# Attention scores: the keys' remainder on all 128 rows, twice, and a second product that takes both parts of the query

## The chip, the core and the metric

The kernel runs on one core of one Trainium2 chip. The engines of the core run side by side, each through its own list of instructions in order: TensorE (PE, with its weight loads shown apart as PEld), VectorE (DVE), ScalarE (ACT), GpSimd (POOL) and SyncE (SP), which issues the transfers. The metric is the time of one execution on the device in microseconds (us); less is better.

## What is computed

Two layers of a backbone with 512 latent tokens and 256 context tokens, each 2048 wide. One projection feeds four groups of heads: a gating MLP, differential attention, a recurrence in two directions, and a short convolution. The change lies in the attention. Each of its four heads has two maps of 64 channels (m), and the two softmaxes are subtracted:

```python
def diff_attn_core(q, k, v, lam):
    s = _f32(jnp.einsum('bqhmd,bkhmd->bhmqk', q, k)) * (HD_QK ** -0.5)
    p = jax.nn.softmax(s, axis=-1)
    a = p[:, :, 0] - lam * p[:, :, 1]
    return jnp.einsum('bhqk,bkhd->bqhd', a.astype(v.dtype), v)
```

In layer 0 the context's queries attend to the 256 context keys and the latents' queries to all 768 keys. In layer 1 only the latents' queries are left.

## The kernel before

Large products are done in float32r, a type of matmul operand that holds a number less finely than float32. So an operand is split in two: a high part (the rounded copy) and a low part, the remainder (the number less its copy). A projection (`mtile`, `mstep`) multiplies three pairs of parts for each of 16 blocks of the contraction: high weights with the high part of h, high weights with the low part, low weights with the high part (line 306, tiles `wh`, `wl`, `h`, result `p`). The weights come by DMA as `wr`, ACT rounds them to `wh` (line 276), and POOL, or DVE for every fourth, subtracts to get `wl` (line 277). There are three buffers of `wh` and of `wl`.

The stages of a layer: the recurrence, then `groups_phase` (four heads of attention, four of the gating MLP, with two convolutions among them in layer 0), then the output projection. In `groups_phase` of layer 0, jobs of `gemv_dve` (line 222, DVE) are spread between the heads.

For one head, `attention` projects the queries and the keys, rotates them (`rot` on PE, line 959, and three elementwise operations, lines 961 to 963), and splits them by map. For map m the rounded channels go to 64 of the 128 rows of `q0` or `q1`, and the remainder of the query to the other 64 rows. Of the keys, `k0` and `k1` hold the rounded channels of their map twice, on both halves of the rows, and the one tile `klo` holds the remainders of both maps, map 0 on rows 0 to 63 and map 1 on rows 64 to 127. So the first product of a tile of scores (line 997) contracts over 128 rows and gives (high + low part of the query) times the high part of the key; the second (line 999) contracts over the 64 rows that `ms` picks, and adds high query times low key in the same PSUM tile `s`.

The loop over 128 queries (`qt`) has six steps in layer 0 (two for the context, with one part of 256 keys) and four in layer 1; a latent step has for each map two parts, 256 and 512 keys. There are 3 buffers of `s`. For each step DVE takes the maxima (lines 1001, 1004, 1005), ACT the exponentials (1008), DVE sums and reciprocals (1011, 1012, 1014), ACT scales the second map (1016), DVE combines both (1017); then PE transposes the result (1025), DVE and ACT copy it (1026), and PE multiplies it with the values (1029). The tile scheduler writes out the order of each engine when the program is built, and puts products of the next projections between the scores and the transposes.

Of the kernel before, what the change touches and what calls it, by code (L numbers as in the profile page):

```python
# [10 lines left out]
F32R = mybir.dt.float32r  # L11
# [92 lines left out]
class Kernel:  # L104
# [840 lines left out]
    def attention(self, l, h):  # L945
        nc, gp, der = self.nc, self.gp, self.der[l]
        V, G, A = nc.vector, nc.gpsimd, nc.scalar
        need_ctx = l < DEPTH - 1
        tT = lambda s, bufs=1, dt=F32: gp.tile([128, T], dt, tag=s, bufs=bufs, name=self.nm(s))

        qk = {}
        for s, c0 in (("q", 1536), ("k", 2048)):
            ctx = need_ctx or s == "k"
            p = self.proj(l, c0 + h * 128, ctx=ctx)
            x = tT("x")
            self.evac(x[:, 0:NCTX], x[:, NCTX:T], p)
            xl = x[:, NCTX:T]
            rp = self.pp.tile([128, 512], F32, tag="pp", name=self.nm("rot"))
            nc.tensor.matmul(out=rp, lhsT=self.rot, rhs=xl, start=True, stop=True)
            rs = gp.tile([128, NLAT], F32, tag="rs", name=self.nm("rs"))  # L960
            V.tensor_tensor(out=rs, in0=rp, in1=self.cs[:, 1, :], op=ALU.mult)
            G.tensor_tensor(out=xl, in0=xl, in1=self.cs[:, 0, :], op=ALU.mult)
            V.tensor_tensor(out=xl, in0=xl, in1=rs, op=ALU.add)
            cs = slice(0 if ctx else NCTX, T)
            t = qk[s] = [tT(f"{s}{m}", dt=F32R) for m in range(2)]
            if s == "k":
                klo = tT("klo", dt=F32R)
            for m, (a, b) in enumerate(((slice(0, 64), slice(64, 128)), (slice(64, 128), slice(0, 64)))):
                A.copy(out=t[m][a, cs], in_=x[a, cs])
                lo = t[m][b, cs] if s == "q" else klo[a, cs]  # L970
                V.tensor_tensor(out=lo, in0=x[a, cs], in1=t[m][a, cs], op=ALU.subtract)
                if s == "k":
                    A.copy(out=t[m][b, cs], in_=t[m][a, cs])
        p = self.proj(l, 2560 + h * 128)
        x = tT("x")
        self.evac(x[:, 0:NCTX], x[:, NCTX:T], p)
        vt = gp.tile([128, 6, 128], F32, tag="vt", name=self.nm("vt"))
        self.transpose6(x, vt, 0, lambda b0, b1, p: A.copy(out=vt[:, b0:b1, :], in_=p[:, 0:b1 - b0, :]))
        sg = self.gate2(gp, self.proj(l, 3072 + h * 128, ctx=need_ctx))

        o = tT("o")
        qt0 = 0 if need_ctx else 2
        for qt in range(qt0, 6):
            isctx = qt < 2
            nk = 2 if isctx else 6
            parts = ((0, NCTX),) if isctx else ((0, NCTX), (NCTX, NLAT))
            np_ = len(parts)
            e = []
            sm = gp.tile([128, 2, 6], F32, tag="sm", bufs=2, name=self.nm("sm"))
            for m in range(2):  # L990
                ms = slice(64 * m, 64 * m + 64)
                qs = slice(qt * 128, qt * 128 + 128)
                sps = []
                for i, (o0, n) in enumerate(parts):
                    s_ = self.sp.tile([128, 512], F32, tag="s", name=self.nm("s"))
                    ks = slice(o0, o0 + n)
                    nc.tensor.matmul(out=s_[:, 0:n], lhsT=qk["q"][m][:, qs], rhs=qk["k"][m][:, ks],
                                     start=True, stop=False)
                    nc.tensor.matmul(out=s_[:, 0:n], lhsT=qk["q"][m][ms, qs], rhs=klo[ms, ks],  # L999
                                     start=False, stop=True)  # L1000
                    V.tensor_reduce(out=sm[:, m, i:i + 1], in_=s_[:, 0:n], axis=AX.X, op=ALU.max)  # L1001
                    sps.append(s_)
                if np_ == 2:
                    V.tensor_tensor(out=sm[:, m, 0:1], in0=sm[:, m, 0:1], in1=sm[:, m, 1:2], op=ALU.max)
                V.tensor_scalar(out=sm[:, m, 2:3], in0=sm[:, m, 0:1], scalar1=-0.125, scalar2=None, op0=ALU.mult)  # L1005
                em = tT(f"e{m}")
                for i, (o0, n) in enumerate(parts):
                    A.activation(out=em[:, o0:o0 + n], in_=sps[i][:, 0:n], func=AF.Exp, scale=0.125,  # L1008
                                 bias=sm[:, m, 2:3], accum_out=sm[:, m, 3 + i:4 + i])
                if np_ == 2:  # L1010
                    V.tensor_tensor(out=sm[:, m, 3:4], in0=sm[:, m, 3:4], in1=sm[:, m, 4:5], op=ALU.add)
                V.reciprocal(out=sm[:, m, 5:6], in_=sm[:, m, 3:4])
                e.append(em)
            V.tensor_tensor(out=sm[:, 1, 5:6], in0=sm[:, 1, 5:6], in1=der["nlam"], op=ALU.mult)
            w = nk * 128
            A.activation(out=e[1][:, 0:w], in_=e[1][:, 0:w], func=AF.Copy, scale=sm[:, 1, 5:6])
            V.scalar_tensor_tensor(out=e[0][:, 0:w], in0=e[0][:, 0:w], scalar=sm[:, 0, 5:6], in1=e[1][:, 0:w],
                                   op0=ALU.mult, op1=ALU.add)
            aT = gp.tile([128, 6, 128], F32, tag="aT", bufs=1, name=self.nm("aT"))
            for b0, b1 in ((0, 2), (2, 6)):  # L1020
                if b0 >= nk:
                    continue
                p = self.pp.tile([128, 4, 128], F32, tag="pp", name=self.nm("atp"))
                for b in range(b0, b1):
                    nc.tensor.transpose(out=p[:, b - b0, :], in_=e[0][:, b * 128:(b + 1) * 128], identity=self.eye)
                (A.copy if b0 else V.tensor_copy)(out=aT[:, b0:b1, :], in_=p[:, 0:b1 - b0, :])
            op = self.pp.tile([128, 512], F32, tag="pp", name=self.nm("op"))
            for b in range(nk):
                nc.tensor.matmul(out=op[:, 0:128], lhsT=vt[:, b, :], rhs=aT[:, b, :], start=(b == 0),
                                 stop=(b == nk - 1))  # L1030
            A.copy(out=o[:, qt * 128:qt * 128 + 128], in_=op[:, 0:128])
        for o0, n in ((0, NCTX), (NCTX, NLAT)):
            if o0 < qt0 * 128:
                continue
            s = slice(o0, o0 + n)
            sq = gp.tile([128, NLAT], F32, tag="rs", name=self.nm("sq"))
            A.activation(out=sq[:, 0:n], in_=o[:, s], func=AF.Square)
            p = self.pp.tile([128, 512], F32, tag="pp", name=self.nm("ssq"))
            nc.tensor.matmul(out=p[:, 0:n], lhsT=self.ones, rhs=sq[:, 0:n], start=True, stop=True)
            A.activation(out=sq[:, 0:n], in_=p[:, 0:n], func=AF.Sqrt, scale=1.0 / 128, bias=self.eps[:, 0:1])  # L1040
            V.reciprocal(out=sq[:, 0:n], in_=sq[:, 0:n])
            V.tensor_tensor(out=o[:, s], in0=o[:, s], in1=sq[:, 0:n], op=ALU.mult)
            V.scalar_tensor_tensor(out=o[:, s], in0=o[:, s], scalar=der["sub"], in1=sg[:, s],
                                   op0=ALU.mult, op1=ALU.mult)
        nc.sync.dma_start(out=self.od[4 + h][:, qt0 * 128:T], in_=o[:, qt0 * 128:T])
# [247 lines left out]
```

## Time and profile before

| | us |
|---|---|
| median of 3 runs | 3791.88 |
| the runs | 3787.84 to 3800.24 |
| the profiled execution, its time on the device | 3795.03 |
| its span, first to last instruction | 3793.2 |
| PE busy in the span | 3508.6 |
| DVE / ACT / POOL busy | 2300.1 / 1866.6 / 1338.5 |

In the views a start is in us from the begin of the span. The duration of a matmul on PE reaches from its start to its modelled end, and matmuls overlap; what one costs in a stream is therefore read as the distance from its start to the start of the next. An x2 in a row of the timeline means two like instructions in a row.

### The profile page before, as it was taken

What the parts mean: (1) busy time and instruction counts of PE and PEld (TensorE: products, weight loads), DVE (VectorE), ACT (ScalarE), POOL (GpSimd) and SP (SyncE); (2) the same over time, 40 slices, a digit from 0 to 9 for tenths busy, and PEclk for the clock granted to TensorE, in tenths of its full rate; (3) what the DMA queues carried; (4) which work ended last, traced back from release to release, by engine and by line L of the source; (5) the groups of instructions that cost most, each with busy time, mean ns of one, the idle gap of its engine ahead of it and who ended that gap; (6) DMA issues with size and microseconds to landing.
All of it is one profiled execution on the core that took longest, in us unless ns stands there. A gap on an engine that the chain in (4) does not pass through costs nothing. (4 is left out here: it accounts for less than half of the span.)

```text
span 3793.2 us, 61920 instructions
## 1 busy us (share of the span) xinstructions
PE 3508.6 (92%) x22388; PEld 2829.0 (75%) x22388; DVE 2300.1 (61%) x4659; ACT 1866.6 (49%) x4131; POOL 1338.5 (35%) x1713
## 2 busy tenths in 40 slices
PE   6999999989999999999897899999778999999998
PEld 1477777767877877888776777777566787777797
DVE  5856777776376536463778734767667526643355
ACT  3466676765234344223324435767666524444454
POOL 2244444544222212222444433445334332222243
PEclk9999999989999999999999999999668999999999
DMA  8432222211343313343655433122011244422565
GB/s 299 181 114 66 58 65 67 62 44 44 104 120 95 98 57 95 109 139 119 201 158 184 124 110 93 55 66 63 27 29 45 64 148 129 123 62 81 158 194 180
DMA packets 239746, 400.89 MB, mean 106 GB/s; under 512 B 25936, under 2 KB 95568, under 8 KB 235344
## 3 DMA queue, kind: packets, MB, share of 16 engines
q1 hardware_dynamic: 232528, 386.45, 33.7%
q10 hardware_dynamic: 6912, 10.49, 0.8%
q8 instruction: 176, 2.88, 0.3%
q14 instruction: 130, 1.06, 0.1%
HBM read 363.28 MB, written 33.56 MB: 105 GB/s over the span
## 5 line engine op out<-in xcount | busy, mean ns | idle before, releaser
L306 PE MATMUL p<-h,wh 128*128 128x512 f32 (+3 forms) x8576 | 2175.9, 351 | 35.9 <-ACT y L1160 10.6
L306 PEld LDWEIGHTS p<-h,wh 128*128 128x128 f32 (+1 forms) x8576 | 1419.7, 191 | 250.6 <-issue 17.8
L306 PE MATMUL p<-h,wl 128*128 128x512 f32 (+2 forms) x4288 | 1350.8, 351 | 39.7 <-DVE wl L277 26.1
L277 POOL TENSOR_TENSOR wl<-wr,wh 128x512 fp32r<-128x512 f32 (+1 forms) x535 | 761.8, 1426 | 1606.5 <-ACT wh L276 1441.6
L276 ACT CAST wh<-wr 128x512 fp32r<-128x512 f32 (+1 forms) x756 | 466.5, 618 | 1001.0 <-PE p L306 792.3
L306 PEld LDWEIGHTS p<-h,wl 128*128 128x128 f32 (+1 forms) x4288 | 751.5, 191 | 143.2 <-DVE wl L277 32.8
L222 DVE SCALAR_TENSOR_TENSOR acc<-gw,sil,acc 128x512 f32<-128x512 f32 (+1 forms) x636 | 449.3, 763 | 33.4 <-DMA gw<-in_w_mod 31.2
L277 DVE TENSOR_TENSOR wl<-wr,wh 128x512 fp32r<-128x512 f32 (+1 forms) x221 | 160.6, 727 | 223.7 <-ACT wh L276 222.1
L804 PEld LDWEIGHTS <-ib 128*128 128x128 f16 x2304 | 133.7, 104 | 138.2 <-issue 70.9
L839 ACT CAST ib<-xa 64x256 f16<-64x256 f32 x480 | 176.4, 368 | 17.5 <-PE xa L809 11.7
L1001 DVE TENSOR_REDUCE sm<-s 128x1 f32<-128x256 f32 (+1 forms) x144 | 76.5, 542 | 102.0 <-PE s L999 99.5
L829 DVE TENSOR_TENSOR T<-inv,c 128x256 f16<-128x256 f32 x240 | 99.1, 413 | 37.0 <-PE inv L804 33.9
L741 POOL TENSOR_SCALAR sp<-SV,pcs 64x64 f32<-64x64 f32 x160 | 80.9, 510 | 108.1 <-DVE SV L762 83.4
L745 PE MATMUL ch<-SV,GM 128*128 128x128 f32 x384 | 90.0, 319 | 17.2 <-DVE SV L762 9.8
L652 POOL TENSOR_TENSOR bk<-t_tw,kr 64x256 f32<-64x256 f32 x96 | 92.7, 966 | 36.8 <-DVE kr L636 33.1
L1008 ACT ACTIVATE e<-s,sm 128x256 f32<-128x256 f32 (+1 forms) x144 | 80.9, 568 | 48.8 <-DVE sm L1005 39.4
L706 PE MATMUL g<-AR,BK 128*128 128x256 f32 (+1 forms) x384 | 96.0, 389 | 3.8 <-DVE BK L658 2.0
L748 PE MATMUL ch<-zs,xb 128*128 128x64 f32 x384 | 81.5, 297 | 15.2 <-ACT zs L747 13.8
L753 PE MATMUL ch<-UV,BKT 128*128 128x128 f32 x352 | 85.5, 328 | 10.2 <-ACT UV L750 9.2
L748 PEld LDWEIGHTS ch<-zs,xb 128*128 128x128 f32 x384 | 65.7, 204 | 38.8 <-ACT zs L747 32.7
L762 DVE SCALAR_TENSOR_TENSOR SV<-ch,pcs,sp 64x64 f32<-64x64 f32 x256 | 72.0, 281 | 36.7 <-PE ch L753 29.0
L835 ACT CAST X<-xa 128x256 f16<-128x256 f32 x192 | 71.4, 372 | 45.5 <-PE xa L809 43.0
(269 smaller groups left out, 5018.9 us busy)
## 6 DMA issues: line engine op xcount, KB each, us to landing
wr<-in_w_in SPq DMA_DIRECT2D x484, 256.0 KB, 2.7
wr<-in_w_out SPq DMA_DIRECT2D x256, 256.0 KB, 2.9
gw<-in_w_mod SPq DMA_DIRECT2D x192, 256.0 KB, 3.0
gw<-in_w_mod SPq DMA_DIRECT2D x32, 1024.0 KB, 6.7
gw<-in_w_mod SPq DMA_DIRECT2D x128, 128.0 KB, 3.1
raw<-rkvd SPq DMA_DIRECT2D x96, 128.5 KB, 2.1
lz<-lzd SPq DMA_DIRECT2D x48, 256.0 KB, 3.1
os<-od SPq DMA_DIRECT2D x32, 256.0 KB, 3.3
```

Of the source, the lines that this page charges most:

```text
L222: self.nc.vector.scalar_tensor_tensor(out=acc, in0=w, scalar=s, in1=acc, op0=ALU.mult, op1=ALU.add)
L276: self.nc.scalar.copy(out=hi, in_=raw)
L277: eng.tensor_tensor(out=lo, in0=raw, in1=hi, op=ALU.subtract)
L306: nc.tensor.matmul(out=p[0:w, 0:n], lhsT=a[:, kk, :], rhs=x[b][k], start=(first and kk == 0 and i == 0), stop=(last and kk == 3 and i == 2))
L652: G.tensor_tensor(out=bk[hs, :, h, :], in0=c4(an)[hs], in1=kn[hs], op=ALU.mult)
L706: nc.tensor.matmul(out=g[:, c], lhsT=bkc(c2 + c), rhs=AR[:, c2 + c, :, 0:nk, :], start=True, stop=True)
L745: nc.tensor.matmul(out=chp[:, 0:128], lhsT=two(GM[:, c, 0]), rhs=two(SV[:, c]), start=True, stop=True)
L748: nc.tensor.matmul(out=chp[:, 128:192], lhsT=XT32[:, c, :], rhs=zs, start=True, stop=True)
L753: nc.tensor.matmul(out=chp[:, 192:320], lhsT=BKT[:, c, :], rhs=two(UV[:, c]), start=True, stop=True)
L804: nc.tensor.matmul(out=out[:, c, :], lhsT=lhsT[:, c, :], rhs=rhs(c), **kw(c))
L829: V.tensor_tensor(out=T1, in0=p1, in1=bt(self.lm(d, j)), op=ALU.mult)
L839: A.copy(out=half(XT, h), in_=aXT[hs])
```

## The change

The keys' remainder gets two tiles, `klo0` and `klo1`, one for each map. DVE writes the 64 rows of the map as before, and a new GpSimd copy repeats them on the other 64 rows. The second product then takes the whole of `q0` or `q1` (128 rows) and the whole of `klo0` or `klo1`: it adds the low part of the query times the low part of the key, which was left out before.

```diff
             if s == "k":
-                klo = tT("klo", dt=F32R)
+                klo = [tT(f"klo{m}", dt=F32R) for m in range(2)]
             for m, (a, b) in enumerate(((slice(0, 64), slice(64, 128)), (slice(64, 128), slice(0, 64)))):
                 A.copy(out=t[m][a, cs], in_=x[a, cs])
-                lo = t[m][b, cs] if s == "q" else klo[a, cs]
+                lo = t[m][b, cs] if s == "q" else klo[m][a, cs]
                 V.tensor_tensor(out=lo, in0=x[a, cs], in1=t[m][a, cs], op=ALU.subtract)
                 if s == "k":
                     A.copy(out=t[m][b, cs], in_=t[m][a, cs])
+                    G.tensor_copy(out=klo[m][b, cs], in_=klo[m][a, cs])
...
-                ms = slice(64 * m, 64 * m + 64)
...
                     nc.tensor.matmul(out=s_[:, 0:n], lhsT=qk["q"][m][:, qs], rhs=qk["k"][m][:, ks],
                                      start=True, stop=False)
-                    nc.tensor.matmul(out=s_[:, 0:n], lhsT=qk["q"][m][ms, qs], rhs=klo[ms, ks],
+                    nc.tensor.matmul(out=s_[:, 0:n], lhsT=qk["q"][m][:, qs], rhs=klo[m][:, ks],
                                      start=False, stop=True)
```

On POOL two copies (line 974) come in for each head, 16 in all. This is POOL in the first head of layer 0, behind the rotation of the keys (line 962), before:

```order
L277 TENSOR_TENSOR wl_12646<-wr_12643,wh_12645 128x512
L277 TENSOR_TENSOR wl_12676<-wr_12673,wh_12675 128x512
L962 TENSOR_TENSOR x_12593<-x_12593,cs_12260 128x512
L277 TENSOR_TENSOR wl_12752<-wr_12749,wh_12751 128x512
L277 TENSOR_TENSOR wl_12782<-wr_12779,wh_12781 128x512
L277 TENSOR_TENSOR wl_12812<-wr_12809,wh_12811 128x512
```

And the same place of the changed kernel:

```order
L277 TENSOR_TENSOR wl_12649<-wr_12646,wh_12648 128x512
L277 TENSOR_TENSOR wl_12679<-wr_12676,wh_12678 128x512
L962 TENSOR_TENSOR x_12593<-x_12593,cs_12260 128x512
L974 COPY klo_2302_12604<-klo_2302_12604 64x768
L974 COPY klo_2303_12605<-klo_2303_12605 64x768
L277 TENSOR_TENSOR wl_12755<-wr_12752,wh_12754 128x512
L277 TENSOR_TENSOR wl_12785<-wr_12782,wh_12784 128x512
L277 TENSOR_TENSOR wl_12815<-wr_12812,wh_12814 128x512
```

The three splits of weights behind the rotation now stand behind the two copies, and the copies stand behind DVE's two subtractions (line 971), which they read.

On PE nothing moves. This is the begin of the scores in the last head of layer 1, before:

```order
L306 MATMUL p_36029<-h_21095,wl_36087 128x512
L997 MATMUL s_36107<-k_6660_35884,q_6641_35747 128x256
L999 MATMUL s_36107<-klo_35886,q_6641_35747 128x256
L997 MATMUL s_36111<-k_6660_35884,q_6641_35747 128x512
L999 MATMUL s_36111<-klo_35886,q_6641_35747 128x512
L997 MATMUL s_36122<-k_6661_35885,q_6642_35748 128x256
L999 MATMUL s_36122<-klo_35886,q_6642_35748 128x256
L306 MATMUL p_36334<-h_20990,wh_36337 128x512
```

And of the changed kernel:

```order
L306 MATMUL p_36053<-h_21107,wl_36111 128x512
L997 MATMUL s_36131<-k_6667_35905,q_6648_35768 128x256
L999 MATMUL s_36131<-klo_6669_35907,q_6648_35768 128x256
L997 MATMUL s_36135<-k_6667_35905,q_6648_35768 128x512
L999 MATMUL s_36135<-klo_6669_35907,q_6648_35768 128x512
L997 MATMUL s_36146<-k_6668_35906,q_6649_35769 128x256
L999 MATMUL s_36146<-klo_6670_35908,q_6649_35769 128x256
L306 MATMUL p_36358<-h_21002,wh_36361 128x512
```

The order is the same; the second product reads another tile, and its operands have 128 rows in place of 64. The orders of DVE, ACT and SP do not change either.

## Rows read from the trace of the kernel before

**Rows 1.** Busy time by stretch: us, PE, PEld, DVE, ACT, POOL, granted clock, DMA.

```profile
1030.00:1480.00 450.00, 437.31 (x2376) 356.95 (x2375) 273.93 (x514) 171.74 (x361) 104.40 (x69) 0.98 0.34 100
3140.00:3450.00 310.00, 304.92 (x1518) 235.18 (x1518) 161.79 (x340) 144.75 (x301) 73.95 (x54) 1.00 0.32 93
```

**Rows 2.** Chain of waits, 3140 to 3450 us: us in total, times, longest.

```profile
DVE sm L1001 <- PE s L999: 49.8, 36, 7.4
```

**Rows 3.** Groups by line and form, whole span: busy us, mean ns.

```profile
L999 PE MATMUL s<-klo,q 64*128 64x512 f32 x64 | 32.1, 502 | 0.0
L999 PE MATMUL s<-klo,q 64*128 64x256 f32 x80 | 30.9, 387 | 0.0
```

**Rows 4.** Timeline of PE: a stretch of products with 256 columns.

```profile
3387.69 0.28 PE L306 MATMUL p<-h,wl 128*128 128x256 f32 x1
3387.81 0.28 PE L306 MATMUL p<-h,wh 128*128 128x256 f32 x1
```

**Rows 5.** Timeline of PE at scores of the last head: start, us.

```profile
3406.51 0.39 PE L306 MATMUL p<-h,wl 128*128 128x512 f32 x1
3406.73 0.28 PE L997 MATMUL s<-k,q 128*128 128x256 f32 x1
3406.94 0.38 PE L999 MATMUL s<-klo,q 64*128 64x256 f32 x1
3407.25 0.49 PE L997 MATMUL s<-k,q 128*128 128x512 f32 x1
3407.68 0.50 PE L999 MATMUL s<-klo,q 64*128 64x512 f32 x1
3408.11 0.39 PE L997 MATMUL s<-k,q 128*128 128x256 f32 x1
3408.42 0.38 PE L999 MATMUL s<-klo,q 64*128 64x256 f32 x1
3408.73 0.74 PE L306 MATMUL p<-h,wh 128*128 128x512 f32 x2
3409.31 0.40 PE L306 MATMUL p<-h,wl 128*128 128x512 f32 x1
3409.55 0.63 PE L306 MATMUL p<-h,wh 128*128 128x512 f32 x2
3410.02 0.39 PE L306 MATMUL p<-h,wl 128*128 128x512 f32 x1
...
3410.93 0.40 PE L997 MATMUL s<-k,q 128*128 128x512 f32 x1
3411.26 0.50 PE L999 MATMUL s<-klo,q 64*128 64x512 f32 x1
```

**Rows 6.** Timeline of the weight loads there.

```profile
3406.51 0.19 PEld L997 LDWEIGHTS s<-k,q 128*128 128x128 f32 x1
3406.94 0.18 PEld L999 LDWEIGHTS s<-klo,q 64*128 64x128 f32 x1 [0.24 <-issue]
```

**Rows 7.** Timeline: the last scores before a transpose, and what it waits for.

```profile
3415.78 0.38 PE L999 MATMUL s<-klo,q 64*128 64x256 f32 x1
...
3418.05 1.02 DVE L1017 SCALAR_TENSOR_TENSOR e<-e,sm,e 128x768 f32<-128x768 f32 x1 [1.11 <-ACT e L1016]
...
3419.21 0.84 PE L1025 MATMUL atp<-cst,e 128*128 128x128 f32 x6
```

**Rows 8.** POOL's nearest operations, whole span, by form.

```profile
L652 POOL TENSOR_TENSOR bk<-t_tw,kr 64x256 f32<-64x256 f32 x96 | 92.7, 966 | 36.8 <-DVE kr L636 33.1
...
L861 POOL COPY GM<-AR 64x256 f32<-64x256 f32 x96 | 40.9, 426 | 130.9 <-PE inv L848 128.1 <-DVE lo L277 0.3
```

**Rows 9.** Timeline, first head of layer 0: DVE, POOL, PE.

```profile
1063.12 0.95 DVE L971 TENSOR_TENSOR klo<-x,k 64x768 fp32r<-64x768 f32 x1
...
1064.66 1.36 POOL L277 TENSOR_TENSOR wl<-wr,wh 128x512 fp32r<-128x512 f32 x1 [11.43 <-ACT wh L276]
...
1067.79 0.40 PE L306 MATMUL p<-h,wl 128*128 128x512 f32 x1
```

## The prediction

> **What bounds the kernel now.** I began with the busy time by stretch, around the two stages in which scores are made: the reader is to see PE at 437 of 450 us in layer 0 and at 305 of 310 us in layer 1, with DVE at 52 to 61%, ACT at 38 to 47% and POOL at 23 to 24%, and a granted clock of 0.98 to 1.00, which is the 2.4 GHz level [rows 1]. The waits agree: in layer 1 DVE's maxima waited 49.8 us in total for the second product of the scores (line 999) [rows 2]. So PE sets the time in these stages, and what a product costs in PE's stream is worth its full price until another chain takes over. The groups give the number of second products: 64 with 512 columns and 80 with 256, together 144 pairs, and their operands are 64 rows high, as nothing next to them is [rows 3].
>
> Then the timeline of PE, read as distances from start to start. In a stream of full-height float32r products one with 256 columns costs 0.12 us (3387.69 to 3387.81) [rows 4], one with 512 columns 0.22 to 0.23 us (3406.51 to 3406.73) [rows 5]. Around the 64-row products the same columns cost more [rows 5]:
>
> - The first product of a pair, behind full-height work: 256 columns 0.21 us (3406.73 to 3406.94), 512 columns 0.33 us (3410.93 to 3411.26). That is 0.09 to 0.10 over the stream.
> - The 64-row product: 256 columns 0.31 us (3406.94 to 3407.25, 3408.42 to 3408.73), 512 columns 0.43 us (3407.68 to 3408.11). That is 0.19 to 0.20 over.
> - The full-height product right behind it: as the first of the next pair it costs 0.43 us with 512 columns (3407.25 to 3407.68) and 0.31 us with 256 (3408.11 to 3408.42), that is 0.19 to 0.20 over, twice what a first product pays when no 64-row product precedes; and a projection's group of two costs 0.58 us (3408.73 to 3409.31) where the next such group costs 0.47 (3409.55 to 3410.02), 0.11 over. So 0.10 to 0.11 belongs to the way out of the 64-row product.
>
> The weight loads show why. The load for the first product starts at 3406.51, as the product before it starts and 0.22 us ahead of its own; the load for the 64-row product starts only at 3406.94, together with its own product, after 0.24 us in which the load side waited for nothing that the profile shows [rows 6]. The change of height stops the stream, twice a pair, and each time a load that is otherwise hidden is laid open.
>
> **The change part by part.** *The second product on 128 rows.* It becomes what line 306 issues in thousands: full height on full height, same type, same columns, into the same PSUM tile as the product before. I price it at the stream's 0.12 and 0.23 us. Then 0.09 + 0.19 + 0.11 = 0.39 us a pair goes. The run of three pairs at 3406.73 says the same: its seven products up to the group at 3408.73 are 0.09 + 0.19 + 0.20 + 0.20 + 0.19 + 0.19 + 0.11 = 1.17 us over the stream, 0.39 a pair [rows 5]. 144 pairs x 0.39 = 56 us. More rows for the same columns are priced at nothing: the first product has 128 rows and needs 0.21 us where the second with 64 rows needs 0.31.
>
> A rule speaks against this. A full-height weight load is seen to start with the product before it, of the same height [rows 5, 6]. The Trainium skill, "TensorE: Matmul & The Clock Gate", Part 3, The mechanism, says that a weight load overlaps products in flight only when its row group differs; two operands of 128 rows share every row group, so by that sentence alone the second load would stay open, and the saving would be near 0 in place of 56 us. The trace disagrees with that reading of it, in the load at 3406.51.
>
> *What is given back.* PE's order is fixed, and the transposes of a step (line 1025) wait for the softmax behind its scores. In the step shown the combination on DVE starts at 3418.05, lasts 1.02 and so ends at 3419.07, and the transposes start at 3419.21; the products put between keep PE occupied up to then, so there is no slack [rows 7]. The chain that ends there begins behind the pair whose second product starts at 3415.78. What PE saves up to that start moves the chain forward too; what it saves behind it (the way out, 0.19 + 0.11 = 0.30 us) does not, and PE will wait that long. There are 4 heads x (6 + 4) = 40 steps. Bounds: 0 if all have slack, and 40 x (0.30 + 0.39) = 28 us if none has and one whole pair more lies behind the start of the chain. I take 14 us, 0.35 a step: near the 0.30 of the row, with a little for the fourth tile of scores, which waits for one of three buffers.
>
> *The copies.* 16 copies of 64 x 768 on POOL, which is at a quarter of its time. The nearest row is POOL's copy of 64 x 256, 426 ns; three times the columns give about 1.3 us. The upper bound is its two-operand operation of that size, 966 ns, so 2.9 us [rows 8]. They cost POOL 20 to 46 us, and PE only if a split of weights behind them comes late. In the first head of layer 0 the second copy can start when DVE has the second remainder, at 1063.12 + 0.95 = 1064.07; at 1.3 us it ends at 1065.4, and the split that now starts at 1064.66 and lasts 1.36 ends at 1066.7. By program order it is first read by the product at 1067.79 [rows 9]. So the copies are hidden there with 1.1 us to spare. At 2.9 us each, and with both only behind 1064.07 (the first needs just the first remainder, so this is more than it can be), they would end at 1069.9 and the split at 1071.2, 3.4 us late; eight heads would give 27 us. I take 0, since a plain copy is what is issued. The scores start tens of us behind this place, so they do not wait for a copy.
>
> **Sum.** 56 - 14 - 0 = 42 us. The profiled execution took 3795.03 us (span 3793.2), which makes 3753. It lies 3.15 us above the median of the runs, 3791.88; against that the forecast is 3791.88 - 42 = **3750 us**, about 1.1% less.
>
> **The rivals.**
>
> - *The softmax chain takes over.* With PE faster, each step runs at the pace of maxima, exponentials and combination, and two or three of a latent step's four pairs are lost to waits. For it: the step of rows 7 has no slack. Against it: DVE and ACT are at about half in layer 1 [rows 1], and DVE's maxima wait for PE, not the other way [rows 2], so the chain itself starts earlier. It would gain 14 to 28 us: 3764 to 3778.
> - *Nothing is gained.* The load of the second product stays open at full height, as by the rule above; the distance from the second product stays at 0.31 and 0.43. Against it are the load at 3406.51 and every pair of products in rows 4 and 5. Time: 3792, within 0.3%.
> - *Slower, by POOL's queue.* The place is the pair of copies ahead of the splits, in every head. To eat 42 us and make the kernel 11 us slower (0.3%, about what a measurement of this kernel can tell from no change), PE would have to stand 53 / 8 = 6.6 us in each head. From 1064.07 to the product at 1067.79 there are 3.7 us, of which the split needs 1.4 [rows 9]; with both copies behind 1064.07 they would have to last 2.3 + 6.6 = 8.9 us, 4.5 each. That is over three times what the nearest copy gives, and above the bound of 2.9. It decides from there on; at 2.5 us each, by the same working, PE stands 2.7 us a head and half of the forecast is gone. Time at 4.5 us: 3803.
>
> **How the numbers follow.** The forecast with its bounds, 28 to 57 us gained (3735 to 3764), gets 0.81; the softmax chain 0.11; nothing gained 0.04; slower 0.02; more than 57 us, if the stream also tightens elsewhere, 0.02. Faster by over 0.3% then holds the first, the second and the last: 0.94; same 0.04; slower 0.02. The range is 3735 to 3768: the bounds of the forecast, with a few us of the chain's case or of late splits at the upper end.
>
> **What would show it.** In the profile after, the distance from a second product to the next start is 0.12 us at 256 columns and 0.23 at 512, and that from a first product too; the weight load of line 999 starts before its product, with no 0.24 us of idle ahead of it. Line 974 has 16 copies on POOL at 1.2 to 1.4 us. The waits show more in front of line 1025, some 0.3 us a step, behind line 1017. The stages named in rows 1 are shorter, with some 56% of the gain in layer 0, which has 80 of the 144 pairs; all others are as they were. What would make it wrong: second products at 0.31 and 0.43 still; a wait for `wl` behind the copies of a microsecond or more in each head; or waits in front of line 1025 or for buffers of `s` that add up to over 28 us.

## The result and the profile after

The changed kernel takes 3745.28 us (median of 4 runs, 3740.13 to 3750.04) against 3791.22 us for the kernel before beside it: a ratio of 0.9875, 95% interval 0.9853 to 0.9896, so 45.9 us or 1.25% less. The forecast was 3750 us.

First the place that was priced, the scores in the last head of layer 1, in the timeline of PE after the change (start, duration in us); it answers to [rows 5]:

```profile
3356.11 0.39 PE L306 MATMUL p<-h,wl 128*128 128x512 f32 x1
3356.33 0.28 PE L997 MATMUL s<-k,q 128*128 128x256 f32 x1
3356.45 0.28 PE L999 MATMUL s<-klo,q 128*128 128x256 f32 x1
3356.57 0.40 PE L997 MATMUL s<-k,q 128*128 128x512 f32 x1
3356.80 0.40 PE L999 MATMUL s<-klo,q 128*128 128x512 f32 x1
3357.03 0.28 PE L997 MATMUL s<-k,q 128*128 128x256 f32 x1
3357.15 0.27 PE L999 MATMUL s<-klo,q 128*128 128x256 f32 x1
3357.26 0.63 PE L306 MATMUL p<-h,wh 128*128 128x512 f32 x2
3357.73 0.39 PE L306 MATMUL p<-h,wl 128*128 128x512 f32 x1
```

Six products take 0.93 us (3356.33 to 3357.26) where they took 2.00 (3406.73 to 3408.73). Every product with 256 columns costs 0.11 to 0.12 us to the next start, every one with 512 costs 0.23, and the projection's group of two costs 0.47 again.

The weight loads of such a pair a little later, which answer to [rows 6] (after the arrow, who ended the idle time of the load side):

```profile
3359.34 0.19 PEld L997 LDWEIGHTS s<-k,q 128*128 128x128 f32 x1 [0.29 <-ACT e L1008]
3359.45 0.19 PEld L999 LDWEIGHTS s<-klo,q 128*128 128x128 f32 x1
```

The second load starts 0.11 us behind the first, while the product that it feeds starts only at 3359.68. It is hidden. The first one shows what was rare before: it waits for an exponential (line 1008), that is for one of the three buffers of `s`, and starts together with its product. In the timeline of PE:

```profile
3359.34 0.50 PE L997 MATMUL s<-k,q 128*128 128x512 f32 x1
3359.68 0.39 PE L999 MATMUL s<-klo,q 128*128 128x512 f32 x1
```

That product costs 0.34 us to the next start, where the one at 3356.57, of the same 512 columns, costs 0.23: a load laid open costs 0.11 us here, with no change of height near it.

By lines 997 and 1029, from the source view by layer (count, min/median/max ns, first and last start), the two score stages can be measured in both kernels. Before:

```profile
L997 PE MATMUL s<-k,q x80: 274/386/628, 1086.2 to 1510.0; 128*128 128x256 f32 x48, 128*128 128x512 f32 x32
L1029 PE MATMUL op<-aT,vt x224: 270/275/377, 1099.6 to 1518.7; 128*128 128x128 f32 x112
L997 PE MATMUL s<-k,q x64: 276/388/495, 3159.3 to 3444.4; 128*128 128x256 f32 x32, 128*128 128x512 f32 x32
L1029 PE MATMUL op<-aT,vt x192: 270/275/377, 3173.7 to 3453.0; 128*128 128x128 f32 x192
```

After:

```profile
L997 PE MATMUL s<-k,q x80: 278/371/498, 1079.9 to 1477.1; 128*128 128x256 f32 x48, 128*128 128x512 f32 x32
L1029 PE MATMUL op<-aT,vt x224: 270/275/377, 1088.1 to 1485.6; 128*128 128x128 f32 x112
L997 PE MATMUL s<-k,q x64: 277/340/505, 3123.5 to 3389.3; 128*128 128x256 f32 x32, 128*128 128x512 f32 x32
L1029 PE MATMUL op<-aT,vt x192: 270/275/377, 3136.4 to 3397.7; 128*128 128x128 f32 x192
```

From the first score to the last product with the values, layer 0 goes from 1518.7 - 1086.2 = 432.5 to 405.7 us and layer 1 from 293.7 to 274.2: together 726.2 to 679.9, 46.3 us less. That is about the whole of the change in the medians (45.9 us). The two profiled executions (3795.03 and 3740.13 us) differ by 54.9; the 8.6 us outside the score stages lie in stages that the change does not touch, and this rest moves about as much between the seven profiles of this study that share PE's order (3058 to 3068 us).

### The profile page after: what moved, and what is told of

Read it like the earlier page. It is cut to its first block, busy times and chain, and to the rows that moved or that the text cites. A ratio compares the mean times of both kernels' runs of the same rounds, so it can differ in the third digit from the quotient of the medians.

```text
span 3738.3 us, 61946 instructions
## 1 busy us (share of the span) xinstructions
PE 3448.6 (92%) x22388; PEld 2811.2 (75%) x22388; DVE 2303.8 (62%) x4659; ACT 1863.0 (50%) x4131; POOL 1364.5 (36%) x1729
## 5 line engine op out<-in xcount | busy, mean ns | idle before, releaser
L222 DVE SCALAR_TENSOR_TENSOR acc<-gw,sil,acc 128x512 f32<-128x512 f32 (+1 forms) x636 | 458.5, 778 | 27.4 <-DMA gw<-in_w_mod 25.1
L745 PEld LDWEIGHTS ch<-SV,GM 128*128 128x128 f32 x384 | 64.4, 204 | 37.6 <-issue 9.3
```

The costliest lines, as they stand in the source:

```text
L222: self.nc.vector.scalar_tensor_tensor(out=acc, in0=w, scalar=s, in1=acc, op0=ALU.mult, op1=ALU.add)
L745: nc.tensor.matmul(out=chp[:, 0:128], lhsT=two(GM[:, c, 0]), rhs=two(SV[:, c]), start=True, stop=True)
```

## The experiments

All ratios are to the kernel before. Beside the times, the table gives the two score stages of each profile, measured as above. Layer 1 is a steadier measure than the whole time; layer 0 is less so, for the clock moves it. `copies_only` has PE's order and products of the kernel before and is 4.5 us shorter there; its granted clock averages 0.996 over that stage, against 0.984 before and 0.992 in the changed kernel, the rest of the time being at the 1.2 GHz level. In the trace before, each of the three stretches at that level begins in a wait of PE of 1.9 to 2.9 us at the begin of a head, or within 1.5 us behind one. By an estimate (the length of the stage times the share that the clock lacks) that is at the most 1.7, 6.8 and 3.4 us, so some 3 of the 46.3 us may be clock and not change; against `copies_only` the two stages are 42.4 us shorter.

| kernel | median us | ratio (95% interval) | layer 0 | layer 1 | both |
|---|---|---|---|---|---|
| before | 3786 to 3791 | 1 | 432.5 | 293.7 | 726.2 |
| changed | 3745.28 | 0.9875 (0.9853 to 0.9896) | 405.7 | 274.2 | 679.9 |
| copies_only | 3785.95 | 0.9997 (0.9982 to 1.0012) | 428.0 | 294.3 | 722.3 |
| zero_half | 3749.53 | 0.9899 (0.9882 to 0.9917) | 406.1 | 275.2 | 681.3 |
| second_twice | 3810.30 | 1.0070 (1.0053 to 1.0087) | 446.1 | 299.3 | 745.4 |
| rows96 | 3741.18 (one run) | | 404.3 | 275.4 | 679.7 |
| no_second | 3736.07 | 0.9861 (0.9824 to 0.9898) | 406.8 | 273.7 | 680.5 |
| copies_twice | 3748.84 | 0.9897 (0.9867 to 0.9926) | 410.2 | 274.7 | 684.9 |
| inverse_rows128 | 3743.82 | 0.9882 (0.9856 to 0.9908) | 408.1 | 274.5 | 682.6 |

Theory 1 is that of the prediction: PE's stream stops when the height of the operands changes between 64 and 128 rows. The rivals say that the gain is from something else in the change, or that a 64-row product is slow by itself.

**One half of the change at a time.** `copies_only` has the tiles and the copies, with the product on 64 rows:

```diff
-                    nc.tensor.matmul(out=s_[:, 0:n], lhsT=qk["q"][m][:, qs], rhs=klo[m][:, ks],
+                    nc.tensor.matmul(out=s_[:, 0:n], lhsT=qk["q"][m][64 * m:64 * m + 64, qs], rhs=klo[m][64 * m:64 * m + 64, ks],
```

> Only half of the change: two tiles of the keys' remainder and the 16 GpSimd copies, but the second product still takes 64 rows. Theory 1 (the change of height stops PE's stream): all 144 pairs keep their 0.39 us, so 3791 us within 5, and the second product still costs 0.31 and 0.43 us to the next start. Rival (the gain comes from something else that the change brings, such as where tiles lie): about 3745. If the copies cost PE time, this run is later than 3791, by up to 27.

It is the kernel before in time (3785.95 us, where the kernel before beside it took 3788.27), and in its last head the second products cost 0.31 to 0.32 us (256 columns) and 0.43 us (512 columns), in the timeline of PE:

```profile
3395.77 0.28 PE L997 MATMUL s<-k,q 128*128 128x256 f32 x1
3395.97 0.38 PE L999 MATMUL s<-klo,q 64*128 64x256 f32 x1
3396.29 0.49 PE L997 MATMUL s<-k,q 128*128 128x512 f32 x1
3396.71 0.50 PE L999 MATMUL s<-klo,q 64*128 64x512 f32 x1
3397.14 0.39 PE L997 MATMUL s<-k,q 128*128 128x256 f32 x1
```

`zero_half` has the product on 128 rows without the copies (the tiles are made once a layer):

```diff
+            for m in range(2):
+                nc.gpsimd.memset(self.klo[m][64 * (1 - m):64 * (1 - m) + 64, :].bitcast(F32), 0.0)
...
-                klo = [tT(f"klo{m}", dt=F32R) for m in range(2)]
+                klo = self.klo
...
-                    G.tensor_copy(out=klo[m][b, cs], in_=klo[m][a, cs])
```

> The other half: second product on 128 rows, but no copies; each tile of the remainder is kept for the layer and its other half is set to zero once, so the low part of the query adds nothing there. Theory 1: 3745 us within 4, with the second product at 0.12 and 0.23 us. If the 16 copies cost the changed kernel time, this run is under 3745, by up to 10 us.

At 3749.53 us it lies just above the forecast of 3745 within 4; its ratio overlaps with that of the changed kernel, and its score stages are within 1.4 us of it. So the taller product alone makes the gain, the copies alone make none, and it does not matter what the other 64 rows hold.

**The copies, doubled.** `copies_twice` repeats the line with `G.tensor_copy`.

```diff
+                    G.tensor_copy(out=klo[m][b, cs], in_=klo[m][a, cs])
```

> The changed kernel with each GpSimd copy made twice (32 in place of 16, some 1.2 us each). If the copies are hidden, 3745 us within 4. If they already hold PE up, 16 x 1.2 = 19 us more, about 3764.

Of 19 us of further work on POOL, 3.6 us appear in the median and 5.0 in the score stages (4.5 of them in layer 0, 0.5 in layer 1), both no more than the runs scatter. The interval of its ratio alone reaches just far enough to hold the 19 us (0.9926); the half of a microsecond in layer 1 leaves no room for it, nor do the waits: PE stands 2.2 us (layer 0) and 1.0 us (layer 1) for `wl` from POOL, each time in the first head of the layer and ahead of its first scores, and in no other head. The copies are nearly hidden.

**What stops the stream.** `second_twice` is the kernel before with the 64-row product issued a second time (line 1001 of that file), which adds the low part of the key twice:

```diff
                     nc.tensor.matmul(out=s_[:, 0:n], lhsT=qk["q"][m][ms, qs], rhs=klo[ms, ks],
+                                     start=False, stop=False)
+                    nc.tensor.matmul(out=s_[:, 0:n], lhsT=qk["q"][m][ms, qs], rhs=klo[ms, ks],
                                      start=False, stop=True)
```

> The kernel before with the 64-row product issued twice in a row (the keys' remainder is added twice). Theory 1: the first of the two follows one of the same height and streams at 0.12 and 0.23 us; 80 x 0.12 + 64 x 0.23 = 24 us of work come in, so 3805 to 3815. Rival (a 64-row product costs 0.31 and 0.43 us wherever it stands): 80 x 0.31 + 64 x 0.43 = 52 us, so 3830 to 3843.

The time is as theory 1 said, but the distances are not. The timeline of PE:

```profile
3415.18 0.28 PE L997 MATMUL s<-k,q 128*128 128x256 f32 x1
3415.38 0.38 PE L999 MATMUL s<-klo,q 64*128 64x256 f32 x1
3415.61 0.28 PE L1001 MATMUL s<-klo,q 64*128 64x256 f32 x1
3415.81 0.50 PE L997 MATMUL s<-k,q 128*128 128x512 f32 x1
3416.24 0.49 PE L999 MATMUL s<-klo,q 64*128 64x512 f32 x1
3416.58 0.39 PE L1001 MATMUL s<-klo,q 64*128 64x512 f32 x1
3416.91 0.38 PE L997 MATMUL s<-k,q 128*128 128x256 f32 x1
```

With 256 columns the first 64-row product costs 0.23 us (3415.38 to 3415.61) and the second 0.20; with 512 columns 0.34 and 0.33. Neither streams at 0.12 and 0.23, and neither costs the 0.31 and 0.43 of the kernel before. Both fit one rule: a change of height, in either direction, costs about 0.09 us at the change, and the product behind the change costs 0.11 us more whatever comes next. The 0.11 is what a load laid open costs in the changed kernel too (3359.34). Here it is the load of the first 64-row product, which starts with its product, in the timeline of the weight loads; the next load starts 0.11 us behind it:

```profile
3415.38 0.18 PEld L999 LDWEIGHTS s<-klo,q 64*128 64x128 f32 x1 [0.24 <-issue]
3415.49 0.19 PEld L1001 LDWEIGHTS s<-klo,q 64*128 64x128 f32 x1
```

What the engine does in the 0.09 us no run shows. In the kernel before a 64-row product is both behind a change and ahead of one, so it bears 0.09 + 0.11 = 0.20 us; here the two halves fall on two products. Each tile of scores has two changes, 0.40 us, with one 64-row product or with two: summed over all of them and the products right behind, the distances lie 62 us over the stream in both traces. (The scheduler orders PE's work a little differently in this kernel, with 18 products of line 306 fewer in the stages, so its stages are no clean measure of the time that came in.)

The Trainium skill, "TensorEngine Tiling (Array Packing)", Key Properties, has this as a drain of the engine at a change of the tiling mode. The runs agree and give its price here.

`rows96` asks whether any other number of rows does it; for map 1 it leaves out half of the rounded query rows:

```diff
-                    nc.tensor.matmul(out=s_[:, 0:n], lhsT=qk["q"][m][:, qs], rhs=klo[m][:, ks],
+                    nc.tensor.matmul(out=s_[:, 0:n], lhsT=qk["q"][m][0:96, qs], rhs=klo[m][0:96, ks],
```

> The changed kernel with the second product on rows 0 to 95 (for map 1 half of the rounded query rows are left out). If any other number of rows stops the stream: 0.31 and 0.43 us for the second product, and 3790 us. If only half the height does, and 96 rows count as full height: 0.12 and 0.23 us, and 3745.

In its one run it is the changed kernel in time, and its timeline of PE has full speed between 128 and 96 rows:

```profile
3358.16 0.28 PE L997 MATMUL s<-k,q 128*128 128x256 f32 x1
3358.28 0.29 PE L999 MATMUL s<-klo,q 96*128 96x256 f32 x1
3358.40 0.40 PE L997 MATMUL s<-k,q 128*128 128x512 f32 x1
3358.64 0.40 PE L999 MATMUL s<-klo,q 96*128 96x512 f32 x1
3358.87 0.28 PE L997 MATMUL s<-k,q 128*128 128x256 f32 x1
```

So theory 1 holds in its narrow form: it is the half height that stops the stream, not just any number of rows that differs: 96, the only other one tried, does not.

**The same cure elsewhere.** `inverse_rows128` tries it on the 64 x 64 products of the recurrence (line 809), on top of the changed kernel:

```diff
-        xs = lambda h, hs, c: XT[hs, c, 64 * h:64 * h + 64]
+        xs = lambda h, hs, c: XT[:, c, 64 * h:64 * h + 64]
...
-        mm1(aXT, lambda h, hs, c: self.eyeh[hs], xs, part(no, no))
+        mm1(aXT, lambda h, hs, c: self.eyeh, xs, part(no, no))
...
-            mm1(aXT, lambda h, hs, c: T1[hs, c, :], xs, part(no, lambda c: j == 5 and c == 3))
+            mm1(aXT, lambda h, hs, c: T1[:, c, :], xs, part(no, lambda c: j == 5 and c == 3))
```

> The changed kernel, and in the inverse of the recurrence the 64 x 64 float16 products (line 809) take all 128 rows, where the other operand is zero on the other half: the same result, 64 columns of weights as before. If the half height alone stops the stream, some 240 groups lose two stops of 0.1 to 0.2 us each, 48 to 96 us of PE's time, of which a stage that often waits for other engines passes on less than half: 3700 to 3730. If the half width of the output stops it too, no change: 3745 within 4.

The time did not move. The groups by form of the changed kernel and, in the second fence, of this one:

```profile
L809 PE MATMUL xa<-ib,T 64*64 64x64 f16 x1920 | 79.5, 205 | 1.4 <-DVE T L829 1.4
```

```profile
L809 PE MATMUL xa<-ib,T 128*64 128x64 f16 x1920 | 80.3, 209 | 1.4 <-DVE T L829 1.4
```

The products are 128 rows high now but still fill 64 columns of the array, and the stop stays: the median distance from the last 128 x 128 product (line 804) to the first of line 809 is 0.123 us in both traces (242 places), where line 804 to itself takes 0.029. It is not the change of line, tile or type: from line 804 with 64 columns to line 306, full height and full width, the median is 0.029 us as well (159 places). The half width stops the stream as the half height does.

**How far PE still sets the pace.** `no_second` leaves out the low part of the key altogether:

```diff
                     nc.tensor.matmul(out=s_[:, 0:n], lhsT=qk["q"][m][:, qs], rhs=qk["k"][m][:, ks],
-                                     start=True, stop=False)
-                    nc.tensor.matmul(out=s_[:, 0:n], lhsT=qk["q"][m][ms, qs], rhs=klo[ms, ks],
-                                     start=False, stop=True)
+                                     start=True, stop=True)
```

> The kernel before without the second product at all: the low part of the key is left out of the scores. Against the changed kernel another 80 x 0.12 + 64 x 0.23 = 24 us of PE's work go. If PE still sets the pace in the score stages of the changed kernel, four fifths or more of that come through: 3722 to 3727. If the softmax chain has taken over there, little does: 3738 to 3745.

It comes out at 3736 us, between the two forecasts. That is 9 us under the changed kernel by the medians and 5 us by the ratios, with intervals that overlap; the score stages are 680.5 us long, no shorter than 679.9. So a gain from a further 24 us of PE's work is not shown. What took its place is only partly known. The scheduler arranges PE's order anew when the products go: other rows move too, and 29 more products of line 306 fall inside the stages, an estimated 5.5 us at the stream's distances. The granted clock over the stage in layer 0 averages 0.975, against 0.992 in the changed kernel, by the same estimate as above up to 7 us more. And the longest wait of PE in layer 0 is then for ACT's copies out of PSUM at the heads' begin:

```profile
PE p L306 <- ACT x L331: 12.1, 2, 6.1
```

In the changed kernel the same wait is 4.8 us. So the run brings in losses of its own and does not tell what PE's pace is still worth; that the softmax holds PE up in most steps is read from the changed kernel itself, in the next section.

## Why the prediction was right

**The saving per pair was right.** 0.39 us x 144 = 56 us was forecast. Summed over all 144 pairs and the products right behind them, the distances from start to start lie 62.2 us over a stream of 0.117 and 0.227 us in the trace before and 7.3 us over it in the trace after: 54.9 us less. (That the two profiled executions differ by the same 54.9 us is chance.) Of the 7.3 us that are left, 4.8 lie at first products with 512 columns, as the one at 3359.34. 80 of the 144 pairs are in layer 0, and 26.8 of the 46.3 us were gained there (58%, forecast 56%; against `copies_only` 22.3 of 42.4, 53%).

**Its division was not.** The prediction read 0.09 us for the way in, 0.19 to 0.20 for the way out, and 0.11 for the product behind it. `second_twice` shows two equal stops of 0.09 + 0.11; the way out seemed dear because the 64-row product pays the second part of its own entry. The sum of a pair is the same, so the forecast did not suffer, but for two 64-row products in a row the prediction's reading gives wrong distances.

**What is given back was priced too high, at the right place.** This is the term of the sum that was mis-sized. 54.9 us of distances became 46.3 us of stage: 8.6 us lost, where 14 were taken (bounds 0 and 28). Over the 40 steps the product ahead of the transposes costs 11.8 us over the stream to their start, 5.0 before: 6.8 us more; the products ahead of first products of scores cost 1.4 us more, the wait for buffers of `s`. These two are 8.2 of the 8.6 us. The sum took 0.35 us for every step, 0.30 of it at the transposes, from one step without slack; there it is 0.17 on average, 0.21 in the 19 steps that had no slack before and 0.13 in the 21 that had some. In the waits of the changed kernel over the whole span, PE's own wait for the combination and the load side's idle time in front of the transposes and the scores are (us in total, times, longest):

```profile
PEld atp L1025 <- issue: 12.4, 22, 1.3
...
PE atp L1025 <- DVE e L1017: 6.7, 15, 1.0
PEld s L997 <- ACT e L1008: 6.1, 21, 0.4
```

The first was 6.3 us before and the second 2.2. The step that answers to [rows 7] now ends like this, in the timeline:

```profile
3363.01 0.28 PE L999 MATMUL s<-klo,q 128*128 128x256 f32 x1
3364.11 0.94 ACT L1016 ACTIVATE e<-e,sm 128x768 f32<-128x768 f32 x1 [1.40 <-DVE sm L1004]
3365.09 1.02 DVE L1017 SCALAR_TENSOR_TENSOR e<-e,sm,e 128x768 f32<-128x768 f32 x1 [0.81 <-ACT e L1016]
...
3366.22 0.64 PEld L1025 LDWEIGHTS atp<-cst,e 128*128 128x128 f32 x6 [0.37 <-issue]
3366.25 0.85 PE L1025 MATMUL atp<-cst,e 128*128 128x128 f32 x6
```

The combination ends at 3366.11 and the transposes start 0.14 us later, as before; the load side stood idle 0.37 us ahead of them, 0.28 before. So this step, from which 0.30 us was read, gives back 0.09: the combination starts 2.08 us behind the last second product where it was 2.27, and most of what the last pair saves reaches the chain too. Counted over all 40 steps, the transposes start within 0.2 us of the end of the combination in 19 before and in 36 after. So the softmax chain has caught up with PE almost everywhere, which the prediction had as a rival: it is there, but it took 8.6 us and not 28 to 42. In the step above the chain itself starts earlier with the scores; that this holds in the other steps is likely from their small waits, but not shown one by one.

**The copies were priced at nothing, and cost about 1 us of waits.** The source view of line 974 in the changed kernel:

```profile
L974 POOL CAST klo<-klo x16: 822/1176/1813, 1053.0 to 3344.9; 64x768 fp32r<-64x768 f32 x16
```

The median of 1.18 us is near the forecast of 1.3. The cover was thinner than the working of [rows 9] had it: in the first head of layer 0 PE's load waits 0.37 us for the split behind the copies, and in layer 1, ahead of the first scores, PE waits 2.7 us for DVE's `wl`, against 1.6 before and 1.5 in `zero_half` (3.4 in `copies_only`). In layer 0 that wait is 2.3 us, against 1.0 and 1.5, but the next one there, for DVE's `sg` (line 345), goes the other way: 1.6 us, against 1.9 and 3.1. Together they are 3.9 us, 2.9 before and 4.6 in `zero_half`, which has no copies, so nothing in layer 0 can be put down to them. The difference of `zero_half` and the changed kernel in the whole time is inside the scatter.

**The rule on weight loads did not decide.** By the sentence of the Trainium skill weighed in the prediction ("TensorE: Matmul & The Clock Gate", Part 3, The mechanism), the second load would have stayed open. The load that starts 0.11 us behind the first, two full-height loads in a row and ahead of its product, speaks against that reading.

No version of the study beats the changed kernel by more than the runs scatter and computes the same; `zero_half` is as fast and needs no copies.

## What to carry to other kernels

When a matmul with a half-height operand stands between full ones, look at the distance from start to start around it, not at its duration: here each change of height cost 0.20 us, so a 64-row product with 256 columns took 0.31 us where one on all rows takes 0.12. Fill the other half with what is at hand; here a copy and zeros gave the same time. And count in the trace how many steps of the next chain have slack before the change: here 21 of 40 had some and in none did the transposes start more than 0.26 us behind the combination afterwards, so that the saving came through less than whole: 46 of 55 us.

## What was not expected of the hardware

- A stop has two parts that fall on two products: 0.09 us at the change of height, and 0.11 us on the product behind it (`second_twice`). The second part is what a load that starts only with its product costs without any change of height (0.34 us against 0.23 at 512 columns, in the changed kernel).
- 96 rows next to 128 rows stream at full speed, 0.12 us at 256 columns (`rows96`).
- Half the width stops the stream as half the height does: 0.123 us against 0.029 us in float16 products of 64 columns, with 64 rows and with 128 (`inverse_rows128`), while full-width products of another line and type follow at 0.029 us.
